# A transformer layer's second feed-forward part: the output norm of the first 384 tokens moved into its loop through DRAM, residual rows in their own buffers, and a row norm in two vector operations

## The chip, the cores and the metric

The kernel runs on one core of a Trainium2 chip. The metric is the device time of one launch in microseconds (us); each figure of the kernel before is from three runs, and one further execution was recorded by the hardware profiler. The core's engines: PE (TensorE, matrix products; PEld are its weight loads), DVE (VectorE), ACT (ScalarE), POOL (GpSimd) and SP (SyncE), whose queue issues every DMA of this kernel. Each engine works through its own queue in order, and semaphores order the engines among each other.

## The reference

One layer for two groups of tokens: 1024 sample tokens and 128 prompt tokens, D = 1024 channels, feed-forward width 4096, everything in fp32. Cut to what matters here (the mixer, a bidirectional mLSTM beside grouped attention, lies ahead of the change):

```
h = x * (1 + sc1) + sh1
mix = mixer(h)                                        # mLSTM, attention, w_out
x = layer_norm(ALPHA * x + g1 * mix, ln1_g, ln1_b)    # the "row norm" below
h = x * (1 + sc2) + sh2
ff = square(relu(h @ w_up)) @ w_down
x = layer_norm(ALPHA * x + g2 * ff, ln2_g, ln2_b)     # the "output norm" below
layer_norm(x) = (x - mean(x)) * rsqrt(var(x) + EPS) * g + b
```

The vectors sh, sc, g come from a conditioning row, one set for the sample tokens and one for the prompt.

## The kernel before

Each fp32 product is made of three: an operand is split into a high part (ACT, L72) and a low part (DVE, L73), and `mm3` issues high x high, high x low, low x high. Nine tiles of 128 tokens: s = 0 to 7 are the sample, s = 8 is the prompt.

**Projection stage (L1079 to 1102).** For each tile in the order `SORD` (tile 5 last) the output projection is multiplied by the gate row (L1096), the residual is added (L1097), and `layer_norm` (L1054) works on the 128 x 1024 rows: two statistics operations and an aggregate on DVE, the inverse root on POOL (`ln_stats`), then (y - mean) * rs on DVE (L1059), * gain on POOL (L1060), + bias on DVE (L1061). The result goes to DRAM as `x1d[s]` and is transposed and modulated (`modulate2`) for the feed-forward part. While the last tile is worked on, the first feed-forward products already run; their banks are freed by a relu on ACT (L1224), with the square on DVE (L1225).

**First feed-forward part: tokens 0 to 383 (tiles 0, 1, 2).** 16 blocks of 256 hidden channels. An up product feeds a down product whose sums stay in six PSUM banks (`dacc`) over all blocks. At the last block `out0_bank` multiplies them by the gate row into three SBUF tiles `y0`.

**Second part: tokens 384 to 1151 (tiles 3 to 8).** Again 16 blocks. The up product of a block uses seven products instead of eight (`up_halves`, L1390, one form of the weights at a time; PSUM banks x, y, p, z, with p and z used twice, so that a later product waits for an addition or a copy that reads the bank: L1379 on DVE, L1393 on ACT, whose outputs `v` and `w` lie in the two buffers of tag `x`). `down` then goes through the six token tiles, two halves of 512 channels each, with four PSUM banks `d`, and adds each bank to `acc` in SBUF (L1189). The up of the next block is issued ahead of the down of a block.

Between the first and the second up of this part stands `out0` for the tiles 0 to 2: it adds the residual row (loaded from `x1d` in halves into tag `x`, L1346), takes statistics (L1347), and `finish` centres on ACT (L1147), scales and shifts on DVE (L1148, L1149), and stores. Its rows of gain and bias stand in `l2a`. When it is through, its SBUF is given to `acc`.

After 14 blocks, `residual` is called for four tiles during the last up (L1133: times gate row; L1138: plus ALPHA times the residual row, in halves, tag `x`). The last `down` takes the last two blocks at once. The tiles in `LATE` get their residual after their sums, the others have it before. ACT takes the statistics of all but the last tile (`stats_act`: L1160, L1162, L1163, with POOL in between, L1161, L1164, L1165) and `finish` ends each tile; the last tile's statistics are taken on DVE (L1195).

The order in each engine's queue is not always that of the code: it is fixed when the program is built, by a list that prefers earlier code and takes an instruction ahead when its operands and its buffers are free. A tag with n buffers lets n tiles of it be in use; the next one waits.

Of the kernel before, what the change touches and what calls it, by code (L numbers as in the profile page):

```python
# [9 lines left out]
F32 = mybir.dt.float32  # L10
# [5 lines left out]
D = 1024  # L16
# [20 lines left out]
def hybrid_step_kernel(  # L37
# [27 lines left out]
    def load(out, in_):  # L65
        nc.sync.dma_start(out=out, in_=in_)
# [140 lines left out]
    def ctile(shape):  # L207
# [12 lines left out]
    gad = {nm: [[dr.tile([128, 2, TB], F32, name=f"{nm}{p}_{b}") for b in range(NTB)] for p in range(4)]  # L220
           for nm in ("om", "gm", "ga")}
    pad = [[dr.tile([128, 2, TB], F32, name=f"pa{p}_{b}") for b in range(NTB)] for p in range(4)]
    x1d = [dr.tile([128, D], F32, name=f"x1d{s}") for s in range(NT)]
    bsd = [[dr.tile([128, 2, 258], F32, name=f"bs{h}_{s}") for s in range(NS)] for h in range(NH)]

# [828 lines left out]
    def layer_norm(y, mk, gain, bias):  # L1054
        st = mk([128, 2, 6], "bst", 2)
        for i in range(2):
            nc.vector.bn_stats(out=st[:, i, :], in_=y[:, 512 * i:512 * i + 512])
        mv, rs = ln_stats(st, mk)
        nc.vector.tensor_scalar(y, y, mv[:, 0:1], rs[:], ALU.subtract, ALU.mult)  # L1059
        nc.gpsimd.tensor_tensor(out=y, in0=y, in1=gain, op=ALU.mult)  # L1060
        nc.vector.tensor_tensor(out=y, in0=y, in1=bias, op=ALU.add)  # L1061

    x1s = {}

# [67 lines left out]
    def residual(mk, acc_s, s, g2):  # L1132
        nc.vector.tensor_tensor(out=acc_s, in0=acc_s, in1=g2, op=ALU.mult)  # L1133
        for half in range(2):
            cs = slice(512 * half, 512 * half + 512)
            x1 = mk([128, 512], "x", 2)
            load(x1[:], x1d[s][:, cs])
            nc.vector.scalar_tensor_tensor(out=acc_s[:, cs], in0=x1[:], scalar=ALPHA, in1=acc_s[:, cs], op0=ALU.mult, op1=ALU.add)  # L1138

    def finish(mk, acc_s, s, l2, nmu, rs, centred, n):  # L1140
        out = y_sample[0, 128 * s:128 * s + 128, :] if s < NS else y_prompt[0]
        w = D // n
        for i in range(n):
            cs = slice(w * i, w * i + w)
            y = acc_s[:, cs]
            if not centred:
                nc.scalar.activation(out=y, in_=y, func=AF.Identity, bias=nmu[:])  # L1147
            nc.vector.scalar_tensor_tensor(out=y, in0=y, scalar=rs[:], in1=l2[0][:, cs], op0=ALU.mult, op1=ALU.mult)  # L1148
            nc.vector.tensor_tensor(out=y, in0=y, in1=l2[1][:, cs], op=ALU.add)  # L1149
            store(out[:, cs], y)  # L1150

    def stats_dve(mk, st):
        mv, rs = ln_stats(st, mk)
        nmu = mk([128, 1], "nmu", 2)
        nc.vector.tensor_scalar(nmu[:], mv[:, 0:1], -1.0, None, ALU.mult)
        return nmu, rs, False
# [14 lines left out]
    def down(mk, acc, toks, fbs, parts, ws, g2, l2, late):  # L1171
        last = g2 is not None
        jk = l2 and l2[2]
        ws = [(parts[i // 2], i % 2, w) for i, w in enumerate(ws)]
        fin = None
        for i, s in enumerate(toks):
            ts_ = slice(128 * i, 128 * i + 128)
            y, gs = acc[:, i, :], g2 and g2[0 if s < NS else 1]
            end = i + 1 == len(toks)
            if last and end:  # L1180
                st = mk([128, 2, 6], "bst", 2)
            for half in range(2):
                cs = slice(512 * half, 512 * half + 512)
                g = psd.tile([128, 512], F32, tag="d", bufs=4, name="d4")
                mm3(g[:], [((a[0][:, m, ts_], a[1][:, m, ts_]), (w[0][:, 0, cs], w[1][:, 0, cs])) for a, m, w in ws])
                if fbs[0] == 0:
                    nc.vector.tensor_copy(out=y[:, cs], in_=g[:])
                elif not last or s in late:
                    nc.vector.tensor_tensor(out=y[:, cs], in0=y[:, cs], in1=g[:], op=ALU.add)  # L1189
                else:  # L1190
                    tm = mk([128, 512], "x", 2)
                    nc.vector.tensor_tensor(out=tm[:], in0=g[:], in1=gs[:, cs], op=ALU.mult)
                    nc.vector.tensor_tensor(out=y[:, cs], in0=y[:, cs], in1=tm[:], op=ALU.add)
                    if end:
                        nc.vector.bn_stats(out=st[:, half, :], in_=y[:, cs])  # L1195
            if last:
                if s in late:
                    residual(mk, y, s, gs)
                if fin:
                    finish(mk, *fin, 1)  # L1200
                fin = (y, s, l2, *(stats_dve(mk, st) if end else stats_act(mk, y, jk)))
        if last:
            finish(mk, *fin, 2)

    def load_l2(l2):
        load(l2[0], ln2_g[0].partition_broadcast(128))
        load(l2[1], ln2_b[0].partition_broadcast(128))
# [68 lines left out]
    def fft(shape, tag, bufs=1, ty=F32):  # L1276
        return (fs if tag in "rx" else ff).tile(list(shape), ty, tag=tag, bufs=bufs, name=tag)

    g2a = fft([128, D], "g20")
    load(g2a[:], gmod[1, 0, :].partition_broadcast(128))  # L1280
    l2a = fft([128, 2, D], "l2a")
    l2a = (l2a[:, 0, :], l2a[:, 1, :])
    load_l2(l2a)


    wuv = kview(w_up)
    ORDER = ("a11", "a22", "a12", "s2", "s1", "s3", "s4")
# [46 lines left out]
    def out0_bank(s):  # L1334
        for half in range(2):
            cs = slice(512 * half, 512 * half + 512)
            nc.vector.tensor_tensor(out=y0[s][:, cs], in0=dacc[s][half][:], in1=g2a[:, cs], op=ALU.mult)

    def out0(s):
        st = fft([128, 2, 6], "bst", 2)  # L1340
        for half in range(2):
            cs = slice(512 * half, 512 * half + 512)
            x1 = fft([128, 512], "x", 2)
            load(x1[:], x1d[s][:, cs])
            y = y0[s][:, cs]
            nc.vector.scalar_tensor_tensor(out=y, in0=x1[:], scalar=ALPHA, in1=y, op0=ALU.mult, op1=ALU.add)  # L1346
            nc.vector.bn_stats(out=st[:, half, :], in_=y)  # L1347
        finish(fft, y0[s], s, l2a, *stats_dve(fft, st), 1)

    ws = [down_w([fb]) for fb in (NFB - 2, NFB - 1)]  # L1350
    pre = up_begin(0)
# [58 lines left out]
            each()  # L1410
        return a

    T1 = (3, 4, 5, 6, 7, 8)
    LATE = T1[:2]
    a = up_halves(pre, aa[0], lambda: None)
    pre = up_begin(1)
    for s in T0:
        out0(s)
    s4f.close()
    ar = pool(st4, "ar", 1)  # L1420
    acc = ar.tile([128, 6, D], F32, name="acc")
    for fb in range(NFB - 2):
# [2 lines left out]
        pre = up_begin(fb + 2)  # L1425
        down(ft, acc, T1, [fb], [a], ws, None, None, ())
        a = nxt
    g2b = [ft([128, D], f"g2{g}") for g in range(2)]
    for g in range(2):
        load(g2b[g][:], gmod[1, g, :].partition_broadcast(128))  # L1430
    todo = list(enumerate(T1))[2:]

    def some1():
        if todo:
            i, s = todo.pop(0)
            residual(ft, acc[:, i, :], s, g2b[0 if s < NS else 1][:])

    nxt = up_halves(pre, aa[1], some1)
    l2 = tp.tile([128, 3, D], F32, tag="t", name="l2")
    l2 = [l2[:, i, :] for i in range(3)]  # L1440
    load_l2(l2)
    down(ft, acc, T1, [NFB - 2, NFB - 1], [a, nxt], down_w([NFB - 2, NFB - 1]), [g[:] for g in g2b], l2, LATE)


# [48 lines left out]
```

## Time and profile before

| | us |
|---|---|
| three runs | 2459.59, 2460.69 (median), 2466.57 |
| profiled execution, its own time | 2459.17 |
| its span, first to last instruction | 2457.4 |
| PE busy | 2360.4 (96%) |
| DVE busy | 1489.1 (61%) |
| ACT busy | 1002.8 (41%) |
| POOL busy | 387.7 (16%) |
| mean granted clock of TensorE | 0.987 |

A row of the profile names a line, an engine, an operation, the tile written, the tiles read, the shape, and a count. A bracket such as [2.29 <-POOL m L1060] says that the engine stood 2.29 us before this instruction, and that POOL's write of `m` at line 1060 ended it. In the windows each engine has its busy time and, in brackets, its number of instructions. The profiler's times are of one execution.

### The profile page before, as it was taken

Reading aid. Unit: us, or ns where it says so; the run is one execution under the profiler, and the core shown is the slowest. Engines: PE = TensorE matmul, PEld = TensorE weight load, DVE = VectorE, ACT = ScalarE, POOL = GpSimd, SP = SyncE. Lnnn points to the kernel's source line nnn. Section 1 sums busy time; section 2 is a strip of 40 time slices with the busy share of each in tenths; the row PEclk is TensorE's granted clock in tenths of the full one; section 3 lists DMA queues with packets and bytes.
Section 4 is the critical chain, followed back from the end, with each engine's and each line's share of the span. In section 5 each row is a group of like instructions: output and inputs, shape, how many; then the busy total and the mean of one; then the engine's idle time right before and its main releaser. Section 6 shows DMA issues by size and latency. Waiting matters only on the chain.

```text
span 2457.4 us, 35978 instructions
## 1 busy us (share of the span) xinstructions
PE 2360.4 (96%) x13293; PEld 2133.9 (87%) x13293; DVE 1489.1 (61%) x2733; ACT 1002.8 (41%) x2136; POOL 387.7 (16%) x575
## 2 busy tenths in 40 slices
PE   6999998999999899899999999999999999999996
PEld 4888787788899899889999999888999889999984
DVE  4745645745655455378787345678444676666676
ACT  3313433534433233256666323225333444444443
POOL 1001110211111011144443000130000221111101
PEclk9999999999999999999999999999999999999998
DMA  7275447545654743520000665334434332222232
GB/s 263 90 200 161 130 127 192 146 125 153 196 154 137 195 151 102 104 67 25 17 16 27 224 189 180 116 120 145 155 120 128 104 103 69 69 69 69 67 96 86
DMA packets 234543, 300.46 MB, mean 122 GB/s; under 512 B 24992, under 2 KB 175600, under 8 KB 234368
## 3 DMA queue, kind: packets, MB, share of 16 engines
q1 hardware_dynamic: 234368, 298.16, 40.2%
q8 instruction: 105, 1.72, 0.3%
q14 instruction: 70, 0.57, 0.1%
HBM read 232.88 MB, written 65.21 MB: 121 GB/s over the span
## 4 chain that ended last, share of the span: by engine, by line
PE 82%; DVE 6%; DMA 6%; ACT 2%; issue 2%; POOL 1%; SPq 0%; DVEq 0%; ACTq 0%; POOLq 0%
PE g L78 13%; PE g L80 12%; PE g L79 12%; PE u L1390 4%; PE d L78 3%; PE d L79 3%; PE d L80 3%; PE pz L1390 2%; PE pp L1390 2%; PE t L872 2%; PE pa L79 2%; PE pa L80 2%; PE pa L78 2%; PE u L78 2%; PE u L80 2%
## 5 line engine op out<-in xcount | busy, mean ns | idle before, releaser
L78 PE MATMUL g<-th,wh 128*128 128x384 f32 x1088 | 372.8, 343 | 9.3 <-DVE fm L248 9.3
L80 PE MATMUL g<-th,wl 128*128 128x384 f32 x1088 | 367.5, 338 | 0.0
L79 PE MATMUL g<-tl,wh 128*128 128x384 f32 x1088 | 365.7, 336 | 0.0
L72 ACT ACTIVATE wh<-raw 128x1024 fp32r<-128x1024 f32 x180 | 188.6, 1057 | 311.7 <-PE d L80 138.3
L73 DVE TENSOR_TENSOR wl<-raw,wh 128x1024 fp32r<-128x1024 f32 x180 | 224.5, 1254 | 123.9 <-ACT wh L72 123.3
L78 PE MATMUL g<-wh,th 128*128 128x512 f32 x600 | 241.2, 402 | 0.5 <-ACT xq L643 0.4
L79 PE MATMUL g<-wl,th 128*128 128x512 f32 x600 | 235.9, 394 | 0.7 <-DVE wl L73 0.7
L80 PE MATMUL g<-wh,tl 128*128 128x512 f32 x600 | 236.1, 394 | 0.0
L78 PEld LDWEIGHTS g<-th,wh 128*128 128x128 f32 x1088 | 205.8, 189 | 18.1 <-DVE fm L248 9.6
L79 PEld LDWEIGHTS g<-tl,wh 128*128 128x128 f32 x1088 | 205.9, 189 | 0.1
L80 PEld LDWEIGHTS g<-th,wl 128*128 128x128 f32 x1088 | 205.3, 189 | 0.4 <-issue 0.4
L1189 DVE TENSOR_TENSOR acc<-acc,d 128x512 f32<-128x512 f32 x160 | 109.9, 687 | 62.9 <-PE d L80 61.0
L78 PEld LDWEIGHTS g<-wh,th 128*128 128x128 f32 x600 | 113.1, 188 | 25.9 <-issue 3.8
L80 PEld LDWEIGHTS g<-wh,tl 128*128 128x128 f32 x600 | 112.9, 188 | 23.4
L79 PEld LDWEIGHTS g<-wl,th 128*128 128x128 f32 x600 | 113.1, 189 | 22.0 <-DVE wl L73 2.3
L72 ACT ACTIVATE ph<-t 128x384 fp32r<-128x384 f32 x192 | 91.0, 493 | 70.4 <-PE t L872 69.9
L248 DVE COPY fm<-g 128x384 f32<-128x384 f32 x96 | 53.3, 555 | 100.1 <-PE g L80 97.9
L73 DVE TENSOR_TENSOR pl<-t,ph 128x384 fp32r<-128x384 f32 x192 | 104.8, 549 | 9.0 <-ACT ph L72 7.2
L1306 POOL TENSOR_TENSOR wtl<-raw 128x512 f32<-128x512 f32 x16 | 23.3, 1454 | 506.7 <-PE pa L79 251.9
L872 PE MATMUL t<-ident,pe 128*128 128x128 f32 x576 | 96.2, 276 | 6.4 <-DVE pl L73 5.5
L78 PE MATMUL u<-th,wh 128*128 128x384 f32 x256 | 86.5, 338 | 2.4 <-ACT r L1224 2.4
L861 POOL TENSOR_SCALAR pe<-pe,rs 128x1152 f32<-128x1152 f32 x64 | 79.0, 1234 | 54.8 <-DVE rs L860 27.0
(393 smaller groups left out, 5921.1 us busy)
## 6 DMA issues: line engine op xcount, KB each, us to landing
raw<-in_w_up_dram SPq DMA_DIRECT2D x64, 512.0 KB
raw<-in_w_down_dram SPq DMA_DIRECT2D x64, 512.0 KB
raw<-in_w_in_dram SPq DMA_DIRECT2D x44, 512.0 KB
kvt<-kvd SPq DMA_DIRECT2D x64, 257.0 KB
raw<-in_w_mod_dram SPq DMA_DIRECT2D x32, 512.0 KB
kvd<-kvs SPq DMA_DIRECT2D x36, 257.0 KB
uw<-ud SPq DMA_DIRECT2D x72, 128.0 KB
bs<-st SPq DMA_DIRECT2D x32, 258.0 KB
```

The costliest lines, as they stand in the source:

```text
L72: nc.scalar.activation(out=hi, in_=src, func=AF.Copy)
L73: nc.vector.tensor_tensor(out=lo, in0=src, in1=f(hi), op=ALU.subtract)
L78: nc.tensor.matmul(out, lhsT=ah, rhs=bh, start=start and i == 0, stop=False)
L79: nc.tensor.matmul(out, lhsT=ah, rhs=bl, start=False, stop=False)
L80: nc.tensor.matmul(out, lhsT=al, rhs=bh, start=False, stop=stop and i == n - 1)
L248: nc.vector.tensor_copy(out=st[:], in_=g[:, 0:TB])
L861: nc.gpsimd.tensor_scalar(pe[:], pe[:], rs[:, 0:1], 1.0, ALU.mult, ALU.mult)
L872: nc.tensor.transpose(pt[:, k, :], pexp[u][:, kt * 128:kt * 128 + 128], ident[:])
L1189: nc.vector.tensor_tensor(out=y[:, cs], in0=y[:, cs], in1=g[:], op=ALU.add)
L1306: nc.gpsimd.tensor_tensor(out=tmp[i], in0=x, in1=y, op=op)
L1390: nc.tensor.matmul(o, lhsT=x[:, k, :], rhs=y[:, k, :], start=fresh and k == 0 and i == 0, stop=k == 3 and i == 2, skip_group_check=True)
```

## The change

In `layer_norm` the three operations with the POOL one between them become two on DVE: (y - mean) * gain, then * rs + bias.

`residual` loads its rows into tag `x1` instead of `x`; `x1` has two buffers in the pool of `acc`.

`out0_bank` also stores each of the three `y0` tiles to DRAM (`y0d`). `out0` no longer runs between the first and the second up: it is called after the down products of blocks 2, 5 and 8, loads `y0d[s]`, and works in halves with tag `x1` for the residual row, the gain row and the bias row one after the other, all on DVE but for the inverse root. `l2a` and its two loads go.

The token tiles of the second part are taken in the order 8, 3, 4, 5, 6, 7 instead of 3 to 8 (each keeps its place in `acc`, so `T1` now has pairs of place and tile), and `LATE` is (8, 3). The sample's gate row is loaded once into tag `g2`, which `out0` also uses for its `y`; the prompt's goes into the third row of `l2`, which ACT's statistics later overwrite.

```diff
--- before.py
+++ after.py
@@ -220,6 +220,7 @@
     gad = {nm: [[dr.tile([128, 2, TB], F32, name=f"{nm}{p}_{b}") for b in range(NTB)] for p in range(4)]
            for nm in ("om", "gm", "ga")}
     pad = [[dr.tile([128, 2, TB], F32, name=f"pa{p}_{b}") for b in range(NTB)] for p in range(4)]
+    y0d = [dr.tile([128, D], F32, name=f"y0d{s}") for s in range(3)]
     x1d = [dr.tile([128, D], F32, name=f"x1d{s}") for s in range(NT)]
     bsd = [[dr.tile([128, 2, 258], F32, name=f"bs{h}_{s}") for s in range(NS)] for h in range(NH)]
 
@@ -1056,9 +1057,8 @@
         for i in range(2):
             nc.vector.bn_stats(out=st[:, i, :], in_=y[:, 512 * i:512 * i + 512])
         mv, rs = ln_stats(st, mk)
-        nc.vector.tensor_scalar(y, y, mv[:, 0:1], rs[:], ALU.subtract, ALU.mult)
-        nc.gpsimd.tensor_tensor(out=y, in0=y, in1=gain, op=ALU.mult)
-        nc.vector.tensor_tensor(out=y, in0=y, in1=bias, op=ALU.add)
+        nc.vector.scalar_tensor_tensor(out=y, in0=y, scalar=mv[:, 0:1], in1=gain, op0=ALU.subtract, op1=ALU.mult)
+        nc.vector.scalar_tensor_tensor(out=y, in0=y, scalar=rs[:], in1=bias, op0=ALU.mult, op1=ALU.add)
 
     x1s = {}
 
@@ -1133,7 +1133,7 @@
         nc.vector.tensor_tensor(out=acc_s, in0=acc_s, in1=g2, op=ALU.mult)
         for half in range(2):
             cs = slice(512 * half, 512 * half + 512)
-            x1 = mk([128, 512], "x", 2)
+            x1 = mk([128, 512], "x1", 2)
             load(x1[:], x1d[s][:, cs])
             nc.vector.scalar_tensor_tensor(out=acc_s[:, cs], in0=x1[:], scalar=ALPHA, in1=acc_s[:, cs], op0=ALU.mult, op1=ALU.add)
 
@@ -1173,10 +1173,10 @@
         jk = l2 and l2[2]
         ws = [(parts[i // 2], i % 2, w) for i, w in enumerate(ws)]
         fin = None
-        for i, s in enumerate(toks):
+        for n, (i, s) in enumerate(toks):
             ts_ = slice(128 * i, 128 * i + 128)
             y, gs = acc[:, i, :], g2 and g2[0 if s < NS else 1]
-            end = i + 1 == len(toks)
+            end = n + 1 == len(toks)
             if last and end:
                 st = mk([128, 2, 6], "bst", 2)
             for half in range(2):
@@ -1278,10 +1278,6 @@
 
     g2a = fft([128, D], "g20")
     load(g2a[:], gmod[1, 0, :].partition_broadcast(128))
-    l2a = fft([128, 2, D], "l2a")
-    l2a = (l2a[:, 0, :], l2a[:, 1, :])
-    load_l2(l2a)
-
 
     wuv = kview(w_up)
     ORDER = ("a11", "a22", "a12", "s2", "s1", "s3", "s4")
@@ -1335,17 +1331,29 @@
         for half in range(2):
             cs = slice(512 * half, 512 * half + 512)
             nc.vector.tensor_tensor(out=y0[s][:, cs], in0=dacc[s][half][:], in1=g2a[:, cs], op=ALU.mult)
+        store(y0d[s][:], y0[s][:])
 
     def out0(s):
-        st = fft([128, 2, 6], "bst", 2)
-        for half in range(2):
-            cs = slice(512 * half, 512 * half + 512)
-            x1 = fft([128, 512], "x", 2)
-            load(x1[:], x1d[s][:, cs])
-            y = y0[s][:, cs]
-            nc.vector.scalar_tensor_tensor(out=y, in0=x1[:], scalar=ALPHA, in1=y, op0=ALU.mult, op1=ALU.add)
-            nc.vector.bn_stats(out=st[:, half, :], in_=y)
-        finish(fft, y0[s], s, l2a, *stats_dve(fft, st), 1)
+        y = ft([128, D], "g2")
+        load(y[:], y0d[s][:])
+        st = ft([128, 2, 6], "bst", 2)
+
+        def halves(src, fn):
+            for half in range(2):
+                cs = slice(512 * half, 512 * half + 512)
+                t = ft([128, 512], "x1", 2)
+                load(t[:], src[:, cs] if src is x1d[s] else src[0, cs].partition_broadcast(128))
+                fn(y[:, cs], t[:], half)
+
+        def first(yc, t, half):
+            nc.vector.scalar_tensor_tensor(out=yc, in0=t, scalar=ALPHA, in1=yc, op0=ALU.mult, op1=ALU.add)
+            nc.vector.bn_stats(out=st[:, half, :], in_=yc)
+
+        halves(x1d[s], first)
+        mv, rs = ln_stats(st, ft)
+        halves(ln2_g, lambda yc, t, half: nc.vector.scalar_tensor_tensor(out=yc, in0=yc, scalar=mv[:, 0:1], in1=t, op0=ALU.subtract, op1=ALU.mult))
+        halves(ln2_b, lambda yc, t, half: nc.vector.scalar_tensor_tensor(out=yc, in0=yc, scalar=rs[:], in1=t, op0=ALU.mult, op1=ALU.add))
+        store(y_sample[0, 128 * s:128 * s + 128, :], y[:])
 
     ws = [down_w([fb]) for fb in (NFB - 2, NFB - 1)]
     pre = up_begin(0)
@@ -1410,12 +1418,10 @@
             each()
         return a
 
-    T1 = (3, 4, 5, 6, 7, 8)
-    LATE = T1[:2]
+    T1 = ((5, 8), (0, 3), (1, 4), (2, 5), (3, 6), (4, 7))
+    LATE = (8, 3)
     a = up_halves(pre, aa[0], lambda: None)
     pre = up_begin(1)
-    for s in T0:
-        out0(s)
     s4f.close()
     ar = pool(st4, "ar", 1)
     acc = ar.tile([128, 6, D], F32, name="acc")
@@ -1425,21 +1431,23 @@
         pre = up_begin(fb + 2)
         down(ft, acc, T1, [fb], [a], ws, None, None, ())
         a = nxt
-    g2b = [ft([128, D], f"g2{g}") for g in range(2)]
-    for g in range(2):
-        load(g2b[g][:], gmod[1, g, :].partition_broadcast(128))
-    todo = list(enumerate(T1))[2:]
+        if fb in (2, 5, 8):
+            out0(fb // 3)
+    g2s = ft([128, D], "g2")
+    load(g2s[:], gmod[1, 0, :].partition_broadcast(128))
+    todo = list(T1[2:])
 
     def some1():
         if todo:
             i, s = todo.pop(0)
-            residual(ft, acc[:, i, :], s, g2b[0 if s < NS else 1][:])
+            residual(ft, acc[:, i, :], s, g2s[:])
 
     nxt = up_halves(pre, aa[1], some1)
     l2 = tp.tile([128, 3, D], F32, tag="t", name="l2")
     l2 = [l2[:, i, :] for i in range(3)]
+    load(l2[2], gmod[1, 1, :].partition_broadcast(128))
     load_l2(l2)
-    down(ft, acc, T1, [NFB - 2, NFB - 1], [a, nxt], down_w([NFB - 2, NFB - 1]), [g[:] for g in g2b], l2, LATE)
+    down(ft, acc, T1, [NFB - 2, NFB - 1], [a, nxt], down_w([NFB - 2, NFB - 1]), [g2s[:], l2[2]], l2, LATE)
 
 
 # ---- launch: one core; inputs and outputs as the reference has them ----
```

## The prediction

> **What bounds the kernel now.** First the page: its head and its chain of work.
>
> ```profile
> PE 2360.4 (96%) x13293; PEld 2133.9 (87%) x13293; DVE 1489.1 (61%) x2733; ACT 1002.8 (41%) x2136; POOL 387.7 (16%) x575
> PE 82%; DVE 6%; DMA 6%; ACT 2%; issue 2%; POOL 1%; SPq 0%; DVEq 0%; ACTq 0%; POOLq 0%
> ```
>
> TensorE sets the time, so only the places where it waits can pay. The table of windows over the stages that the diff touches finds them (columns: width, busy of PE, PEld, DVE, ACT, POOL, granted clock, DMA share, GB/s), and the table of waits of TensorE from 1560 us on names the releasers.
>
> ```profile
> 1560.00:1660.00 100.00, 100.00 (x484) 84.60 (x483) 71.37 (x119) 24.33 (x44) 32.34 (x26) 1.00 0.32 106
> 1660.00:1680.00 20.00, 16.59 (x83) 15.26 (x82) 15.28 (x23) 9.44 (x18) 3.26 (x1) 0.91 0.42 132
> 1924.74:2010.41 85.67, 79.19 (x397) 72.10 (x397) 66.51 (x101) 41.23 (x75) 19.47 (x16) 0.98 0.35 117
> 2000.00:2375.00 375.00, 374.75 (x1886) 339.68 (x1886) 261.00 (x364) 155.50 (x288) 68.49 (x48) 1.00 0.22 71
> 2382.40:2440.00 57.60, 50.54 (x229) 43.88 (x227) 37.92 (x52) 24.86 (x41) 4.94 (x10) 0.91 0.27 92
> 2440.00:2457.40 17.40, 0.00 (x1) 0.00 (x0) 12.42 (x18) 5.38 (x9) 2.88 (x7) 0.61 0.30 121
> ```
>
> ```profile
> PE pz L1390 <- ACT x L1393: 7.1, 1, 7.1
> PE pp L1390 <- ACT y L1147: 4.7, 1, 4.7
> PE u L78 <- ACT r L1224: 2.4, 1, 2.4
> PE u L195 <- ACT r L1224: 1.0, 1, 1.0
> ```
>
> Each wait belongs to one part of the change: L1224 to the end of the row norm (B), L1147 to the output norm of the first 384 tokens (A), L1393 to the residual buffers (C). From 2000 to 2375 TensorE is full: nothing to gain there, something to lose. The steady round of the second part gives the measure (chain of waits: start, length, what).
>
> ```profile
> 2041.38 6.27 PE u L1390 x36
> 2047.65 2.08 PE pp L1390 x12
> ...
> 2072.36 6.27 PE u L1390 x36
> ```
>
> A round is 30.98 us (2072.36 - 2041.38). The seven up products take 6.27 + 4 x 2.08 = 14.6, the down products the other 16.4.
>
> **A, the norm of tokens 0 to 383.** The window 1924.74 to 2010.41 holds three ups and two downs, 3 x 14.6 + 2 x 16.4 = 76.6 us. It took 85.67: 9.1 lost, 6.5 of it idle, the rest at a lower clock. The cause is the 16.8 us of DVE and 3.5 us of ACT that the norms push into the second up (tile y; minimum, median, maximum ns).
>
> ```profile
> L1346 DVE SCALAR_TENSOR_TENSOR y<-x,y x6: 685/686/694, 1942.2 to 1954.0; 128x512 f32<-128x512 f32 x6
> L1347 DVE BATCH_NORM_STATS2 bst<-y x6: 643/686/692, 1943.3 to 1955.1; 128x6 f32<-128x512 f32 x6
> L1148 DVE SCALAR_TENSOR_TENSOR y<-y,brs,l2a x3: 1272/1278/1284, 1950.4 to 1960.4; 128x1024 f32<-128x1024 f32 x3
> L1149 DVE TENSOR_TENSOR y<-y,l2a x3: 1208/1222/1222, 1952.2 to 1962.0; 128x1024 f32<-128x1024 f32 x3
> L1147 ACT ACTIVATE y<-y,nmu x3: 1148/1154/1155, 1948.8 to 1958.9; 128x1024 f32<-128x1024 f32 x3
> ```
>
> By these rows it is 8.2 + 7.5 us of DVE, and 1 for aggregates and means. The change adds a 512 KB store behind each tile's gate products (L1337), which DVE does just before the ups, by 1925.5. SP's next entries (SP timelines, all with 0.3 to 0.4 us of SP each) are
>
> ```profile
> 1936.46 0.34 SPq L66 DMA_DIRECT2D raw<-in_w_down_dram  x1
> 2043.64 0.38 SPq L66 DMA_DIRECT2D raw<-in_w_up_dram  x1
> 2388.69 0.33 SPq L66 DMA_DIRECT2D l<-in_ln_g_dram  x1
> ```
>
> and the first of them is 11 us later: three stores delay nothing. `acc` now waits for these stores, over 20 us ahead of its first use near 1954 (1924.74 + 2 x 14.6). I take 8.5 of the 9.1; ends 4 and 9.1, since DVE may still be filled there (first rival).
>
> The norms come back inside the loop. For each tile: eight half operations like L1346 or L1347, 8 x 0.69, and 0.2 for the aggregate, 5.7 us of DVE; two small POOL operations; no ACT; on SP one 512 KB load, six of 256 KB, one store. DVE is busy 261.00 of 375, so a round has 9.4 us free: the work fits. What can cost is DVE standing at a load with evictions queued behind it. Such a stand, from DVE's timeline in the last up:
>
> ```profile
> 2402.45 0.69 DVE L1138 SCALAR_TENSOR_TENSOR acc<-x,acc 128x512 f32<-128x512 f32 x1 [2.75 <-DMA x<-x1d]
> ```
>
> Four banks of 1.36 us (16.4 / 12) stand between the down products and their eviction: a stand of about 2.7 us is borne there. In the up, the product after next needs the sum of this one (L1379), 2.08 - 0.55 = 1.5 us of slack. A stand of 2.7 in the worst place costs 1.2; nine pairs of loads give at most 11, less the first pairs, loaded ahead: ends 0 and 8. I take 1.5, nearer to 0, since the stands fall anywhere in the round, not always in its worst place. SP is no bound in itself:
>
> ```profile
> SPq L66 <- DVE wl L73: 194.7, 24, 13.5
> SPq L66 <- DVE uf L73: 153.6, 24, 9.7
> ```
>
> It stands at weight buffers for 348 of 375 us, so it has time; the weights come long before their use (rival 3). Bytes: 2 MB loaded and 0.5 stored for each tile. Even in one round (2.1 MB now, share 0.22) that is a share near 0.5; the stage from 1680 to 1900 ran at 0.44 with TensorE busy 220.00 of 220.
>
> **B, the row norm.** DVE and TensorE at the last of the nine tiles:
>
> ```profile
> 1659.63 0.81 DVE L1059 TENSOR_SCALAR m<-m,bmv,brs 128x1024 f32<-128x1024 f32 x1 [0.73 <-POOL brs L1051]
> 1660.58 3.26 POOL L1060 TENSOR_TENSOR m<-m 128x1024 f32<-128x1024 f32 x1 [0.98 <-PE u L80]
> 1663.87 1.23 DVE L1061 TENSOR_TENSOR m<-m 128x1024 f32<-128x1024 f32 x1 [2.29 <-POOL m L1060]
> 1668.63 0.52 PE L78 MATMUL u<-th,wh 128*128 128x384 f32 x1 [2.43 <-ACT r L1224]
> 1672.15 0.40 PE L80 MATMUL u<-th,wl 128*128 128x384 f32 x1
> ```
>
> Out go 0.81 and 1.23 of DVE and 3.26 of POOL; in come two operations of the form of L1148, 1.28 each. DVE gets 0.52 us more work in each tile, and loses two stands, 0.73 (the first operation needs no `rs`) and 2.29: the queue behind, with the square (L1225) whose lateness holds ACT and so the relu, moves 2.5 us ahead. In the first eight tiles TensorE is 100.00 of 100: nothing. At the last it lost 2.43, then 1.6 at half pitch (eleven products in 3.52 us, where full pitch takes 1.9), then 1.0 at L195: 5.0. A move of 2.5 ends the first wait and with it the slow stretch, but what follows waits on weights; I take 3.0, ends 0 and 5.0.
>
> [...]
>
> **C, the residual rows.** From 2382.40 the work is one up and two downs, 14.6 + 2 x 16.4 = 47.4; the window is 57.60 wide: 10.2 lost. The up's `v` (L1393) and the rows of `x1d` share two buffers `x`; `w` holds one, so the rows come one by one (chain of waits, then ACT's timeline):
>
> ```profile
> 2396.33 2.65 DMA x<-x1d
> 2399.72 2.70 DMA x<-x1d
> ...
> 2409.79 0.49 ACT L1393 ACTIVATE x<-pz 128x384 f32<-128x384 f32 x1 [17.97 <-DVE acc L1138]
> ```
>
> With `x1` apart, `v` follows its product at once, near 2393, and the last product needs no wait. Eight half rows in two buffers come in pairs, some 3.4 us apart: done by about 2390 to 2395, while DVE, with 37.92 of 57.60, has room. I take 9.5, ends 6 and 10.2.
>
> Then the tail, 17.4 us behind TensorE's end. ACT's statistics go tile by tile (ACT and POOL timelines):
>
> ```profile
> 2421.70 1.06 ACT L1160 ACTIVATE l<-acc 128x1024 f32<-128x1024 f32 x1 [4.84 <-DVE acc L1138]
> ...
> 2446.29 0.57 POOL L1165 TENSOR_TENSOR brs<-brs,mhalf 128x1 f32<-128x1 f32 x1
> ```
>
> Five tiles take 25.2 us, and 10.5 more follow to the end at 2457.4. They started 18.3 before TensorE's end at 2440.0, since at the restart 36 of 144 products were done but no tile. Without the wait, on the old clock: the last product ends at 2397.0; 24 products of the first of the two blocks (four banks, 5.5 us) cover `u2`'s way through DVE and ACT, about 3.5; the first tile's banks are full at 2405.2 (12 products more), its residual takes 3.3 of DVE, statistics start at 2408.5, 21.3 before an end at 2429.8. That is 3.0 more of a head start: tail 14.4. I take 3; ends 0, and 6.9 if DVE finishes the last tile while ACT is on the one before.
>
> At nothing: tile 8 first, whose bank needs the last product's half, is covered by those 24 products. Its gate row goes into `l2`, whose loads start at 2388.69 in the trace; first use is near 2404, and 512 KB at twice the 2.7 of 256 KB are there by 2394. The two `l2a` loads go away unseen.
>
> **Sum**, against the profiled execution (2459.17 us, span 2457.4): A -8.5, loop +1.5, B -3.0, C -9.5, tail -3.0: -22.5, so 2436.7. The median of the three runs is 1.5 above that execution: 2438.
>
> **The rivals.** (1) The norms come back where they were. A queue does not run in the order of the code but takes what has its buffers: the gate rows that stand behind the loop (L1430) were loaded ahead of its second round.
>
> ```profile
> 1966.30 0.97 SPq L66 DMA_DIRECT2D g<-gmod  x2
> ```
>
> So the first `out0` can be pulled into the second up. For it: the stores land near 1930. Against: its operations now stand behind those of the up, and without the norms DVE is busy 66.51 less 16.8 us of 85.67, which leaves room. Price: all of A: 2446. (2) Own buffers don't free the path, because DVE goes on standing at `x1d` with the up's sums behind it. For it: the 2.75 above. Against: pairs, of which the first is there ahead. With three pairs and 2 us each: 2444. (3) Slower: SP. Loads and the store of `out0` stand in the one queue with the weights; a store that waits for DVE holds them. A weight load issued at 2043.64 feeds products from 2072.36 on, so an SP stand costs nothing until it passes some 20 us; then one for one. Slower than before from 22.5 us lost, 7.5 in each of the three rounds: stands of 28 us, where three load pairs and their arithmetic come to about 3 x 3.4 + 5.7 = 16. Stands of 30 us: 2438 + 30 = 2468. (4) The row norm costs DVE. Nine tiles at 0.52 are 4.7 us of DVE work; if DVE were what the stage waits for, B would be +4.7 instead of -3.0: 2446. Against: DVE is at 71.37 of 100 while TensorE is at 100.00.
>
> [...]
>
> **How the numbers follow.** Forecast 0.62, rivals (1) 0.13, (2) 0.10, (4) 0.05, (3) 0.06, and 0.04 for losses of several kinds that leave about nothing. A measurement of this kernel tells 0.3%, 7 us, from no change: faster is below 2453. The forecast, (1), (2) and (4) are all there but for their outer edges: 0.88 faster, 0.07 the same, 0.05 slower. The forecast's own range: with A, B, C and the tail at their far ends, -9.1 - 5.0 - 10.2 - 6.9 + 0 gives 2429 on the median; the near ends, -4 - 0 - 6 - 0 + 8, give 2459, but not all at once; half of that way is 2448. The whole range takes in (1), (2), (4): 2430 to 2451.
>
> **What the changed profile would show.** A: no wait L1390 on L1147, and the fourth up starts near 2002, less what B gives, instead of 2010.41. Loop: TensorE at least 373 of 375 in its rounds; DVE near 278. B: no wait of DVE on POOL's 3.26, and the wait on L1224 below 0.6. C: the wait on L1393 gone, the window from the last up to TensorE's end 48 to 50 wide; the tail 11 to 15. Wrong if TensorE waits on DVE in the rounds with `out0` for more than 8 us in all, if SP's longest stand on a weight buffer grows past 25, or if the tail stays at 17.

## The result, and the profile after

The changed kernel takes 2440.4 us (median of 4 runs, 2439.24 to 2442.41) where the kernel before takes 2461.89 beside it: a ratio of 0.9911, 95% interval 0.9894 to 0.9928. Timed again later, beside three of the experiments, it was 2433.52 against 2458.26: 0.9898 (0.9884 to 0.9911). The profiled execution took 2440.70 us (2459.17 before), its span 2438.9.

The page after, busy time and chain of work:

```profile
PE 2360.1 (97%) x13293; PEld 2135.6 (88%) x13293; DVE 1495.6 (61%) x2736; ACT 999.8 (41%) x2133; POOL 366.6 (15%) x566
PE 84%; DVE 6%; DMA 6%; ACT 2%; issue 1%; POOL 1%; SPq 0%; DVEq 0%; ACTq 0%; POOLq 0%
```

TensorE's work is the same, and it waits less. The windows over the same stages (columns as in the prediction), and TensorE's waits from 1560 us on:

```profile
1560.00:1660.00 100.00, 100.00 (x478) 83.87 (x477) 74.35 (x116) 22.30 (x43) 13.91 (x16) 1.00 0.30 101
1660.00:1680.00 20.00, 20.00 (x113) 18.99 (x112) 16.98 (x27) 11.74 (x20) 1.73 (x2) 1.00 0.42 132
1923.86:2003.13 79.27, 77.92 (x398) 70.48 (x397) 67.20 (x103) 37.63 (x72) 16.82 (x16) 1.00 0.53 174
2000.00:2375.00 375.00, 375.00 (x1887) 340.03 (x1886) 265.62 (x372) 156.07 (x289) 69.34 (x48) 1.00 0.24 75
2375.03:2423.61 48.58, 47.66 (x229) 41.17 (x227) 38.96 (x52) 26.35 (x43) 6.19 (x12) 1.00 0.33 120
2423.61:2438.90 15.29, 0.00 (x1) 0.00 (x0) 11.23 (x16) 4.07 (x7) 2.76 (x6) 0.65 0.26 103
```

```profile
PE d L78 <- DVE acc L1187: 1.0, 1, 1.0
PE d L78 <- ACT ab L72: 0.9, 1, 0.9
PE d L78 <- DVE acc L1189: 0.3, 1, 0.3
```

All four waits of before (7.1, 4.7, 2.4, 1.0) are gone; 2.2 us of small ones are left. The granted clock is 1.00 in every stage that was at 0.91 or 0.98.

To compare many profiles, four marks on TensorE's timeline: P, the first product `t<-pkh,pqh` of the attention; U0, the first product `u` of the second part; LU, that of its last up; E, the end of the last product. (Line numbers of the changed kernel lie 1 higher from L223 to the row norm, are those of before again from there to L1278, and lie 8 higher at the ups: L1390 is L1398, L1393 is L1401, L1379 is L1387. e6 and e8 lie 1 higher still behind L1203, e7 behind L1060, and e1 lies 1 lower than before there. The marks are rounded to 0.1 us ahead of the differences.)

| kernel | P | P to U0 | U0 to LU | LU to E | E to end | span |
|---|---|---|---|---|---|---|
| before | 1065.6 | 859.0 | 457.8 | 57.6 | 17.4 | 2457.4 |
| before_again | 1066.6 | 858.8 | 457.7 | 56.5 | 17.6 | 2457.1 |
| after | 1070.2 | 853.5 | 451.2 | 48.7 | 15.3 | 2438.9 |
| after_again | 1062.7 | 853.9 | 451.2 | 47.9 | 15.3 | 2431.0 |
| e1_ln_only | 1060.9 | 853.8 | 458.4 | 55.6 | 17.6 | 2446.2 |
| e10_ln_three_dve | 1064.0 | 856.0 | 458.7 | 57.4 | 17.4 | 2453.5 |
| e2_c_only | 1060.4 | 858.9 | 458.8 | 49.4 | 15.4 | 2442.9 |
| e7_a_only | 1066.4 | 858.8 | 450.0 | 59.1 | 18.6 | 2452.9 |
| e5_out0_early | 1064.8 | 853.5 | 457.3 | 48.9 | 15.6 | 2440.1 |
| e6_out0_behind | 1064.5 | 853.9 | 452.3 | 49.2 | 15.3 | 2435.1 |
| e9_out0_x | 1064.7 | 854.1 | 449.6 | 49.6 | 15.3 | 2433.3 |
| e8_best | 1062.6 | 854.1 | 451.1 | 49.6 | 19.8 | 2437.3 |
| e11_late8 | 1061.9 | 854.0 | 449.6 | 48.7 | 15.5 | 2429.7 |
| e4_tile3_first | 1065.0 | 854.0 | 450.9 | 47.8 | 15.1 | 2432.8 |

P lies ahead of everything that was changed, and every engine's order up to it is the same in before and after; it moves between 1060.4 and 1070.2 all the same, by 7.5 us between two executions of one kernel; why is not known. One row of the tile `t` from each of the two profiles of the changed kernel:

```profile
L78 PE MATMUL t<-pkh,pqh x4: 222/273/277, 1070.2 to 1071.2; 128*128 128x128 f32 x4
```

```profile
L78 PE MATMUL t<-pkh,pqh x4: 223/272/276, 1062.7 to 1063.7; 128*128 128x128 f32 x4
```

So spans of single executions can't be compared to better than some 8 us, and stages behind P can: P to U0 repeats within 0.6 us, U0 to LU within 1.2, the last up within 2.

### The profile page after: what moved, and what is told of

It reads as the page before. It is cut to its first block, busy times and chain, and to the rows that moved or that the text cites. A ratio compares the mean times of both kernels' runs of the same rounds, so it can differ in the third digit from the quotient of the medians.

```text
span 2438.9 us, 35985 instructions
## 1 busy us (share of the span) xinstructions
PE 2360.1 (97%) x13293; PEld 2135.6 (88%) x13293; DVE 1495.6 (61%) x2736; ACT 999.8 (41%) x2133; POOL 366.6 (15%) x566
## 4 chain that ended last, share of the span: by engine, by line
PE 84%; DVE 6%; DMA 6%; ACT 2%; issue 1%; POOL 1%; SPq 0%; DVEq 0%; ACTq 0%; POOLq 0%
PE g L78 13%; PE g L80 13%; PE g L79 13%; PE u L1398 4%; PE d L78 3%; PE d L79 3%; PE d L80 3%; PE pz L1398 2%; PE pp L1398 2%; PE t L873 2%; PE u L80 2%; PE u L78 2%; PE u L79 2%; PE pa L79 2%; PE pa L80 2%; PE pa L78 2%
## 5 line engine op out<-in xcount | busy, mean ns | idle before, releaser
L73 DVE TENSOR_TENSOR wl<-raw,wh 128x1024 fp32r<-128x1024 f32 x180 | 224.1, 1252 | 126.3 <-ACT wh L72 125.5
L73 DVE TENSOR_TENSOR pl<-t,ph 128x384 fp32r<-128x384 f32 x192 | 104.8, 549 | 9.0 <-ACT ph L72 7.2
L1302 POOL TENSOR_TENSOR wtl<-raw 128x512 f32<-128x512 f32 x16 | 21.2, 1324 | 487.4 <-PE pa L79 252.7
L78 PE MATMUL pv<-ph,vh 128*128 128x256 f32 x288 | 85.6, 297 | 1.5 <-DVE tl L73 1.5
```

The lines of the kernel that those rows point to most:

```text
L73: nc.vector.tensor_tensor(out=lo, in0=src, in1=f(hi), op=ALU.subtract)
L78: nc.tensor.matmul(out, lhsT=ah, rhs=bh, start=start and i == 0, stop=False)
L1302: nc.gpsimd.tensor_tensor(out=tmp[i], in0=x, in1=y, op=op)
```

## The experiments

### One part at a time

B alone, in the kernel before:

```
-        nc.vector.tensor_scalar(y, y, mv[:, 0:1], rs[:], ALU.subtract, ALU.mult)
-        nc.gpsimd.tensor_tensor(out=y, in0=y, in1=gain, op=ALU.mult)
-        nc.vector.tensor_tensor(out=y, in0=y, in1=bias, op=ALU.add)
+        nc.vector.scalar_tensor_tensor(out=y, in0=y, scalar=mv[:, 0:1], in1=gain, op0=ALU.subtract, op1=ALU.mult)
+        nc.vector.scalar_tensor_tensor(out=y, in0=y, scalar=rs[:], in1=bias, op0=ALU.mult, op1=ALU.add)
```

> The kernel before with the row norm in two DVE operations alone (part B). If the parts add up, it gains what the stage from the first attention product (L872/L873) to the first up of the second part gained in the changed kernel, 866.3 to 860.9: 5.5 us, so about 2456.5 against 2461.9; the prediction's own term was 3.0, about 2459. PE should be full in the window 1660 to 1680 of the profile (16.59 of 20 before). Rival (4), DVE sets the stage: 9 x 0.52 = 4.7 us slower, 2466.6. Rival from the traces: the 5.5 are a variation like the 4.6 us that the two profiles differ by ahead of the attention, and nothing is left, 2462.

C alone, in the kernel before (the new token order and the single gate row go with it, since `x1` needs their room):

```
-            x1 = mk([128, 512], "x", 2)
+            x1 = mk([128, 512], "x1", 2)
...
-    T1 = (3, 4, 5, 6, 7, 8)
-    LATE = T1[:2]
+    T1 = ((5, 8), (0, 3), (1, 4), (2, 5), (3, 6), (4, 7))
+    LATE = (8, 3)
...
+    load(l2[2], gmod[1, 1, :].partition_broadcast(128))
```

> The kernel before with part C alone: the residual rows in buffers x1, one gate row for tokens 384 on and the row for the last tile in l2, tile 8 first. The stretch from the last up to the end of TensorE should go from 57.60 to the 48.58 of the changed kernel (9.0), the tail from 17.4 to 15.3 (2.1): 11 us, about 2451. Rival (2), DVE stands at the rows all the same: 6 us of it come back, 2457. Rival: the parts lean on one another (the norms in the transition hold what C needs): anything but 11.

A alone: the changed kernel with the old row norm, and in `residual` and `out0`

```
-            x1 = mk([128, 512], "x1", 2)
+            x1 = mk([128, 512], "x", 2)
...
-                t = ft([128, 512], "x1", 2)
+                t = ft([128, 512], "x", 2)
```

> The changed kernel with the old row norm, and with the residual rows and the half rows of out0 back in the two buffers x: part A alone (with the order of the tiles and the single gate row as changed). If the parts add up, the stretch from the first up to the fourth gains the 6.4 us of the changed kernel (85.67 to 79.27) and the wait of TensorE on ACT at v (L1401) is there again with some 7 to 10: about 2455.5. Rival: the half rows of out0 hold the buffers that v needs, in the transition too: less than 3 gained, 2459 or more. The prediction's own term was 8.5 less 1.5.

And nothing at all:

> The kernel before once more, as the measure of what a profile differs by with no change at all. If the 4.6 us by which the first attention product starts later in the changed kernel's profile (1058.4 and 1063.0) are variation, this profile has it anywhere from 1058 to 1063, and its span follows; if they come from the change, it is at 1058.4 within 1. Time: 2461.9 within 2.

Against 2457.95 for the kernel before on that chip: B 2452.05 (0.9979, 0.9970 to 0.9988), C 2448.00 (0.9960, 0.9947 to 0.9972), A 2452.86 (0.9982, 0.9973 to 0.9991), nothing 2458.09 (1.0002, 0.9993 to 1.0010). The product of the three is 0.9921. That is inside the first interval of the changed kernel (0.9894 to 0.9928) but outside the second (0.9884 to 0.9911), and 0.0023 above its 0.9898, where 0.001 had been set as the mark: the parts add up but for some 3 us that A alone loses at the end (below), which C takes away. With these, 0.0012 of the whole, the product is 0.9909, inside both intervals.

The null run has P at 1066.6, 1 us from before, but the table shows what P does otherwise; the 4.6 us by which the first two profiles differ ahead of the attention are variation.

Each part acts in its own column. B takes P to U0 from 858.9 to 853.8 and nothing else. C takes the last up and the tail, together, from 75.0 and 74.1 to 64.8. Its two windows, from LU and from E:

```profile
2378.11:2427.50 49.39, 48.01 (x229) 41.33 (x227) 39.14 (x53) 26.51 (x43) 6.19 (x12) 1.00 0.33 118
2427.50:2442.90 15.40, 0.00 (x1) 0.00 (x0) 11.22 (x16) 4.07 (x7) 2.79 (x6) 0.62 0.25 102
```

A takes U0 to LU from 457.7 to 450.0, and pays 3 of the 7.7 back at the end, where `v` still shares its buffers with the residual rows: TensorE's wait there is 8.7, longer than the 7.1 of before, and the tail is 1 longer too. Since this kernel has the new token order and the single gate row and still waits, it is the buffers `x1` of C that remove the wait.

```profile
PE pz L1399 <- ACT x L1402: 8.7, 1, 8.7
```

### What the row norm's gain is made of

The kernel before, with one word changed in the gain's line: `nc.gpsimd` to `nc.vector`.

> The kernel before with the gain of the row norm multiplied on DVE instead of POOL: three DVE operations (0.81 + 1.22 + 1.22 = 3.3 us for each tile, where before has 2.0 on DVE and 3.26 on POOL, and the two operations of the change 2.6). It tells what part B's gain came from. If it is the round by way of POOL that went (0.73 and 2.29 of standing at the last tile), this kernel gains nearly what e1 did: the stage to the first up of the second part 854 to 855 us against 858.9 (e1: 853.8), 4 to 5 us. If DVE's work counts (rival 4), it is 9 x 1.2 = 11 us more of it and the gain shrinks or turns. If only the last tile counts, it lies 0.7 behind e1.

It measured 2455.28 against 2458.07 (0.9991, 0.9982 to 1.0000), by time at the edge of what can be told; P to U0 is 856.0, short of the 854 to 855 that was expected. Of B's 5.1 us, 2.9 come from the gain leaving POOL, though DVE then does 1.2 us more for each tile, and 2.2 from the two-operation form, which has both less work (2.6 for 3.3 us in each tile) and shorter stands at `brs` (0.8 us in all for 6.7); these two were not taken apart. The waits of DVE from 1560 to 1680 us tell why, in before, in this kernel, and in the changed one:

```profile
DVE m L1061 <- POOL m L1060: 20.9, 9, 2.7
DVE m L1059 <- POOL brs L1051: 6.8, 9, 1.0
DVE m L1096 <- PE g L80: 5.8, 8, 3.3
```

```profile
DVE m L1096 <- PE g L80: 10.7, 7, 2.1
DVE m L1059 <- POOL brs L1051: 6.7, 9, 1.0
```

```profile
DVE m L1096 <- PE g L80: 24.2, 9, 3.3
DVE m L1061 <- POOL brs L1052: 0.8, 1, 0.8
```

Before, DVE stood at POOL 27.7 us in nine tiles. In these 120 us it is busy for 71.37 + 15.28 = 86.7 (the prediction's first two windows); with the stands that is 114.4, and what is left is about its wait for the projection's products, 5.8: its only spare time. In this kernel that wait is 10.7 and in the changed one 24.2. At the last tile this kernel still has a wait, the one for the relu, of 1.85 us:

```profile
1672.39 0.66 PE L195 MATMUL u<-ident,m 128*128 128x128 f32 x4 [1.85 <-ACT r L1224]
```

That is most of its distance to e1 (856.0 - 853.8 = 2.2), where TensorE is busy 20.00 of 20.

### Where the output norms stand

> The changed kernel once more, as the mark for the three kernels beside it. The parts alone measured 0.9979 (row norm), 0.9960 (residual rows) and 0.9982 (output norms); if they add up, their product is 0.9921, about 2438.5 where before is 2457.95. If they lean on one another, the ratio is off that by more than 0.001.

After it, e5: `out0` for the tiles 0, 1, 2 is called ahead of the second up.

```
+    for s in T0:
+        out0(s)
     for fb in range(NFB - 2):
...
-        if fb in (2, 5, 8):
-            out0(fb // 3)
```

> The changed kernel with the three output norms issued together ahead of the second up, where they stood before, but in the new form (gate products through DRAM, eight half operations on DVE, none on ACT). It tells whether place or form brings part A. If place counts (DVE must not carry 15 us between the evictions of the second up and the ups behind it), the first up to the fourth takes some 85 again, +6 us on the changed kernel. If form counts (no ACT operation and no operation of 1.28 between the evictions), it stays near the 79.27 of the changed kernel: 0 to +2. Rival (3): one buffer g2 holds one tile, so each tile waits for a load of 2.7 us behind the store of the one ahead; DVE stands with the evictions behind it: +5 and more.

And e6, where DVE's queue is forced to the order of the code:

```
-            out0(fb // 3)
+            with tc.issue_after(ev.ins):      # ev: the last addition to acc of this block
+                out0(fb // 3)
```

> The changed kernel with the DVE operations of each output norm tied behind the last eviction of rounds 2, 5 and 8 (an order on DVE's queue), so that they stand where the code has them and not in the first rounds, where DVE did them in the changed kernel. The run of part A alone, in which shared buffers kept them in the rounds, had 77.72 us from the first up to the fourth against 79.27, and TensorE busy 371.96 of 372 behind it. Theory: 1.5 us faster than the changed kernel, no loss in the rounds. Rival, the prediction's loop term: 1.5 to 8 us lost in the rounds, since the rows stand with evictions behind them; then it is equal or slower. Rival: the ratio to the changed kernel lies below what can be told, 0.1%.

Last e9: the changed kernel with `out0`'s half rows in the up's buffers `x`, the residual's staying in `x1`.

```
-                t = ft([128, 512], "x1", 2)
+                t = ft([128, 512], "x", 2)
```

> The changed kernel with the half rows of out0 in the buffers x that the up's w and v use, the residual rows staying in x1. In the run of part A alone the shared x kept the output norms in the rounds, at 449.8 us from the first up of the second part to its last, where the changed kernel took 451.17 and 451.19 with the norms done in the first rounds, and before 457.8. Theory (the norms cost in the transition what they cost nothing of in the rounds): about 450 here, and the 64 us of the changed kernel from the last up to the end: 1.3 us faster than the changed kernel, ratio about 0.9895 to 0.9905. Rival: with the residual rows apart the scheduler places them otherwise than in that run; then 451 to 454 as in e6, where they stood in the rounds and cost 2.9.

On one chip: after_again 2433.52, e5 2441.95 (0.9928, 0.9914 to 0.9943), e6 2436.33 (0.9906, 0.9892 to 0.9921). On another chip e9 2434.26 (0.9902, 0.9889 to 0.9916). The changed kernel, e6 and e9 can't be told apart by time. By the stage from U0 to LU e9 can: 449.6, and 449.6 again in e11, against 451.2 twice in the changed kernel. e6 can't: 452.3, and 451.1 in e8 (below), which has the same order up to the last up.

In the changed kernel the norms are not in rounds 2, 5 and 8. All three stand in the first rounds (DVE's timeline, first row of each tile and the last of all):

```profile
1933.74 1.29 DVE L1349 SCALAR_TENSOR_TENSOR g<-x,g 128x512 f32<-128x512 f32 x2
...
1965.50 0.68 DVE L1349 SCALAR_TENSOR_TENSOR g<-x,g 128x512 f32<-128x512 f32 x1
...
1985.73 1.29 DVE L1349 SCALAR_TENSOR_TENSOR g<-x,g 128x512 f32<-128x512 f32 x2 [1.95 <-DMA g<-y0d]
...
2002.83 0.75 DVE L1355 SCALAR_TENSOR_TENSOR g<-g,brs,x 128x512 f32<-128x512 f32 x1
```

That is the first rival's mechanism, at a fifth of its price. e5 shows that the price hangs on rank. Its first tile starts 10 us behind U0, as in the changed kernel, the second at 30 instead of 42, the third at 54 instead of 62, in the same light form, and it takes 6.1 us more from U0 to LU: nearly all of the 6.6 that A gained there. The window and the waits of the transition in e5:

```profile
1918.49:2004.00 85.51, 80.21 (x397) 72.32 (x397) 69.73 (x104) 37.72 (x72) 16.25 (x16) 0.96 0.53 179
```

```profile
PE u L1398 <- DVE uf L73: 3.5, 2, 3.1
PE pp L1398 <- DVE u L1387: 1.3, 1, 1.3
```

Standing ahead of the up in the code, the norms are preferred to the splits of the up's weights (L73), and TensorE waits for those. DVE's and TensorE's rows ahead of the longest wait in e5:

```profile
1953.95 3.45 DVE L1354 SCALAR_TENSOR_TENSOR g<-g,bmv,x 128x512 f32<-128x512 f32 x2
1957.33 1.61 DVE L73 TENSOR_TENSOR ab<-r,ab 128x384 fp32r<-128x384 f32 x1
1958.87 1.28 DVE L73 TENSOR_TENSOR uf<-raw,uf 128x512 fp32r<-128x512 f32 x2
```

```profile
1959.60 0.69 PE L1398 MATMUL u<-tfa22h,uf 128*128 128x384 f32 x1 [3.14 <-DVE uf L73]
```

Rank is not the whole of this wait: the two L1354 took 3.45 us instead of 2 x 0.75, and the split behind them 1.61 instead of 0.55, while POOL made sums of the up's weights (L1302, three of 1.5 to 1.6 us from 1953.67 to 1958.52). How much of the 6.1 is this collision was not taken apart. Standing behind, the norms fill DVE's gaps. So the ACT operations that the new form saves are not what A lives on (at the old place the new form takes 457.3, the old one 457.8); place is.

In e9 the shared `x` holds them back into the rounds (2014, 2107 and 2200 us), and there they cost nothing (window of e9 from 1990 to 2365 us; DVE is at the 278 that the prediction gave for the rounds):

```profile
1990.00:2365.00 375.00, 374.94 (x1885) 339.50 (x1884) 278.09 (x393) 155.43 (x288) 73.90 (x54) 1.00 0.29 89
```

In e6, with the order forced, the same work in nearly the same rounds costs 2.7 us against e9, and 1.5 in e8. In e6 two rounds together take 63.79 instead of 61.94 (chain of waits of e6), and between them that chain runs through the load of a bias row, DVE, and a load of `w_down` that was issued late behind them:

```profile
1996.10 6.27 PE u L1399 x36
...
2033.09 3.87 DMA x<-in_ln_b_dram
...
2042.32 5.62 DMA raw<-in_w_down_dram
...
2059.89 6.27 PE u L1399 x36
```

### The end

By these rows the tail hangs on DVE: in the changed kernel ACT stands for it at the fourth tile, and the last bank, which TensorE left at 2423.6, is added at 2428.56 (timelines of ACT and DVE).

```profile
2419.05 1.06 ACT L1160 ACTIVATE l<-acc 128x1024 f32<-128x1024 f32 x1 [2.94 <-DVE acc L1193]
```

```profile
2428.56 0.67 DVE L1193 TENSOR_TENSOR acc<-acc,x 128x512 f32<-128x512 f32 x1
```

Two ways to unload DVE. e8 is e6 and, in `finish`,

```
-            nc.vector.tensor_tensor(out=y, in0=y, in1=l2[1][:, cs], op=ALU.add)
+            (nc.gpsimd if s in (8, 3, 4) else nc.vector).tensor_tensor(out=y, in0=y, in1=l2[1][:, cs], op=ALU.add)
```

> The kernel of e6, and the bias rows of the first three tiles of the last down (8, 3, 4) added on POOL in place of DVE (L1149). In the changed kernel DVE is the full engine of the end: its last bank is added at 2428.56, 5 us behind TensorE's end, and ACT stands 2.94 us at DVE at 2419.05. Theory: three operations of 1.22 us off DVE bring the tail 15.3 down by 2 to 3.6 us. Rival: POOL takes 3.2 us for each (the row of the old row norm), its small operations for the next tile stand behind that, and ACT's statistics come later: nothing gained, or 1 to 3 lost. Rival: the tail hangs on ACT's statistics (5 us for each tile), then nothing moves.

e11 is e9 with

```
-    LATE = (8, 3)
+    LATE = (8,)
...
-    todo = list(T1[2:])
+    todo = list(T1[1:])
```

> The kernel of e9 with the residual row of tile 3 added in the last up too (tile 8 alone is late): 2.6 us of DVE (L1133 1.22, L1138 2 x 0.69) leave the last down, 1.4 (two more L1192) come in. Theory, DVE is behind TensorE at the end by 5 us (its last bank is added at 2428.56, TensorE ended at 2423.6): the tail goes from 15.3 to about 14. Rival: tile 3 then needs its gate row product ahead of the sums, the five residual rows no longer fit the last up, and TensorE waits there: 1 to 3 us lost.

Neither shortened the tail. e8 took 2440.17 (0.9926, 0.9914 to 0.9939), 3.8 more than e6, and its tail is 19.8. DVE's additions that start while POOL works stretch to three times their length (timelines of DVE and POOL in e8):

```profile
2402.93 0.68 DVE L1192 TENSOR_TENSOR x<-d,g 128x512 f32<-128x512 f32 x1
2403.64 2.19 DVE L1193 TENSOR_TENSOR acc<-acc,x 128x512 f32<-128x512 f32 x1
...
2408.49 2.40 DVE L1193 TENSOR_TENSOR acc<-acc,x 128x512 f32<-128x512 f32 x1
```

```profile
2402.49 2.79 POOL L1149 TENSOR_TENSOR acc<-acc,l 128x1024 f32<-128x1024 f32 x1
2407.94 2.41 POOL L1149 TENSOR_TENSOR acc<-acc,l 128x1024 f32<-128x1024 f32 x1
```

Each ends 0.5 us behind POOL's. So DVE lost 4.7 us in three such stretches (2.19 + 2.40 + 2.17 - 3 x 0.69) for 3.7 saved, and the statistics of the next tile wait behind POOL besides. e11 took 2433.27 (0.9900, 0.9887 to 0.9914), its tail 15.5: DVE had 1.2 us less to do and stood 4.6 us at the inverse roots (L1148) where it stood 3.7 in the changed kernel. In its queue the scaling of the tile before stands ahead of the next additions, and waits for that tile's statistics; taking work away there made it wait longer. So that DVE's work sets the tail is not shown; its order may. Whether another order in this queue would shorten the tail was not tried.

Tile 3 ahead of tile 8 (and the statistics' work row in a buffer of its own):

```
-    T1 = ((5, 8), (0, 3), (1, 4), (2, 5), (3, 6), (4, 7))
-    LATE = (8, 3)
+    T1 = ((0, 3), (5, 8), (1, 4), (2, 5), (3, 6), (4, 7))
+    LATE = (3, 8)
```

> The changed kernel with tile 3 ahead of tile 8 in the second part's downs (and the work row of ACT's statistics in a buffer of its own, since the third row of l2 is then in use longer). The prediction priced tile 8 first at nothing, its first bank being covered by 24 products (5.5 us against 3.5 for the last half of the up). Theory: from the last up to TensorE's end 48 to 49 and the tail 15 to 16, as in the changed kernel, within 0.5. Rival: tile 8 first costs the 0.9 us that TensorE waited for ACT's ab in the changed kernel, and this kernel is 1 us faster.

2435.23 (0.9908, 0.9894 to 0.9921); 47.8 and 15.1, where the two profiles of the changed kernel have 48.7 and 47.9, and 15.3. The wait for `ab` is not in it, and it is 0.2 (after_again) to 1.6 (e9) in profiles that have tile 8 first, 0.9 in the first one of after. So tile 8 first may cost up to some 1.5 us; it can't be told by time.

## Why the prediction was right, and where its steps were off

The forecast was 2438 us, in 2430 to 2451; 2440.4 was measured, and 2433.5 later. The sum was -22.5; by the table (before and before_again against after and after_again) the columns behind P give -5.2, -6.6, -8.7 and -2.2, together -22.7. The median moved by 21.5 in the first comparison and by 24.7 in the second. That the sum is so close is partly luck: B was put 2.2 too low, and the other terms 2.0 too high together.

- **B** said -3.0 and is -5.2. The step that failed is "a move of 2.5 ends the first wait [...], but what follows waits on weights". Nothing waited on weights: TensorE is full from 1660 to 1680. And the queue moved further: the last tile's third operation (L1061) started 598.3 us behind P, the changed kernel's second one 592.9 (1663.13 - 1070.2), 5.3 earlier. The prediction took the stands of the last tile alone and read "DVE at 71.37 of 100" as room. Of the 120 us it was busy 86.7 and stood 27.7 at POOL; the stands of the tiles ahead had made DVE late before the last norm came. DVE's last product with the gate row (L1096) started 590.1 us behind P in before, without a wait, and 587.0 behind P in the changed kernel, after a wait for TensorE: 3.0 of the 5.3 were there by then (DVE's timelines, one row of before, two of after).

```profile
1655.69 0.67 DVE L1096 TENSOR_TENSOR m<-g,m 128x512 f32<-128x512 f32 x1
```

```profile
1657.27 0.69 DVE L1096 TENSOR_TENSOR m<-g,m 128x512 f32<-128x512 f32 x1 [0.60 <-PE g L80]
...
1663.13 1.28 DVE L1061 SCALAR_TENSOR_TENSOR m<-m,brs 128x1024 f32<-128x1024 f32 x1
```

- **A and loop** said -8.5 and +1.5, -7.0 together; -6.6 was measured. The parts are otherwise than put: what failed is that the norms would stand in the rounds. They were pulled forward (rival 1) and cost 1.6 there (451.2 against 449.6 in e9), about what had been put for the rounds, by luck. With the norms truly in the rounds the first step holds, 457.7 to 449.6 being 8.1, and the loop costs 0 (e9), 1.5 (e8) or 2.7 (e6), within its ends of 0 and 8.
- **C** said -9.5: LU to E went from 57.6 and 56.5 to 48.7 and 47.9, -8.7. The wait on L1393 is gone, and no wait on `x1d` took its place (rival 2): the window is 48.58, in the 48 to 50 named. Of the 1.2 above 47.4 that are left, 0.9 is the wait for `ab`, which the prediction took to be covered.
- **Tail** said -3.0, 14.4; it is 15.3, -2.2. The head start is more than was reckoned: ACT's statistics begin at 2401.82, 21.8 ahead of 2423.61. What was missed is that they do not run on at 5 us for each tile; the fourth waits 2.94 for DVE. The end that the prediction gave for DVE, 6.9, presumed DVE had nothing to catch up on.
- **Rival (3)**, SP: the stands on weight buffers in the rounds stay as they were, the longest 13.5, in the changed kernel and in e9, where the norms are in the rounds.
- **Rival (4)**: DVE's work in the stage rose from 71.37 to 74.35, and its standing at POOL fell from 27.7 to 0.8. The work's direction is as the rival has it, two operations of 1.28 in each tile for 0.81 (L1059) and 1.23 (L1061); it does not bear on the stand. e10, with 81.42 of DVE in its own such window, still takes 2.9 us less from P to U0 than before.

On the clock: before_again stood 2.5 us at the relu as before did 2.43, and the granted clock in the 20 us around is 0.91 in both; e10 stood 1.85 and has 1.00 (its window 1658 to 1678). The length of the stand alone does not part the cases, though. Ahead of the change TensorE in before stood 1.81 us (to 627.41) and had 0.53 from 627.57 to 630.98; in e11 it stood 2.03 us (to 625.06) and had 1.00 up to 634. What brings the lower clock is not shown.

## What to carry to other kernels

An engine's busy share tells its room only together with what it stands for: add the stands from its table of waits, and look for the wait that is true spare time (here the 5.8 us at the projection's products). Where an operation stands in the order of the code can matter more than how light it is: the same norms ahead of the next up cost 6 us more than as filling behind it, and holding them to one place by a forced order cost more (1.5 to 2.7 us) than letting shared buffers do it (nothing). When single executions of a kernel differ by 8 us ahead of the change, compare stages from a mark behind that.

## What was not expected of the hardware

In e8 a DVE addition with both inputs in SBUF (L1193, 128 x 512) that started while POOL added two 128 x 1024 fp32 tiles took 2.19 and 2.40 us instead of 0.69, and ended 0.5 us behind POOL's end; L1192, which reads one input from PSUM, kept 0.68 beside it. Why is not shown. It shows in e5 as well (above), in the changed kernel (L1354 took 1.80 us from 1972.01 instead of 0.75, POOL's L1302 1.29 from 1971.97), and, the other way round, in the row norm of before, where it was POOL that took longer:

```profile
L1060 POOL TENSOR_TENSOR m<-m x9: 2397/3249/3308, 1563.9 to 1660.6; 128x1024 f32<-128x1024 f32 x9
```

The 2.40 us are those of the first tile, when no DVE operation was under way at its start; the other eight took 3.25 to 3.31, each with a split of DVE's (L73, 1.22 us) begun about 0.2 us ahead. By that one tile an estimated 0.85 us (3.25 - 2.40) of each of these eight stands of DVE at POOL came from DVE's own work beside it.
